# A hybrid-attention layer on one core: a later place in the order for the joining copies, gate units spread anew over the heads, and the last head's weights transposed on TensorE

## The chip, the core and the metric

One core of one Trainium2 chip runs the whole layer as one program. The metric is the device time of one execution in microseconds (us); lower is better. In the profile, PE is TensorE (PEld its weight loads), ACT is ScalarE, DVE is VectorE, POOL is GpSimd and SP is SyncE, whose queue issues most of the DMA transfers. Each engine works through its own list of instructions in order.

## The reference, cut to what matters

The input `x` has 512 rows of 2048 features. One combined projection of the normalised input gives queries, keys, values and a SiLU gate path for three branches of four heads each (head width 128), and merge gates of width 2048 for each branch.

```python
def hybrid_layer(x, norm_g, w_in, ...):
    hn = rmsnorm(x, norm_g)
    proj = jnp.einsum('bsd,dc->bsc', hn, w_in)
    br = proj[..., :QKVG_COLS].reshape(b, s, N_BRANCH, 4, BRANCH_W)
    gates = jax.nn.sigmoid(proj[..., QKVG_COLS + N_HEADS:] + b_gate).reshape(b, s, N_BRANCH, D_MODEL)
    ya = forgetting_attention(rmsnorm(q), rmsnorm(k), v, f_logit)       # branch A: causal softmax with a forget bias
    yb = chunked_relpos_attention(rmsnorm(q), rmsnorm(k), v, rel_bias)  # branch B: softmax over a band
    yc = stick_breaking_attention(q, k, v)                              # branch C: causal, in log space
    ys = jnp.stack([from_heads(ya), from_heads(yb), from_heads(yc)], axis=2)
    ys = ys * jax.nn.silu(br[:, :, :, 3])
    up = jnp.einsum('bsnw,nwd->bsnd', ys, w_up)
    merged = jnp.sum(gates * up, axis=2)
    return x + jnp.einsum('bsd,de->bse', merged, w_out)
```

In each head the attention weights `p` (512 queries by up to 512 keys, in blocks of 128 by 128, of which ten lie on or below the diagonal) are multiplied with the values. On TensorE that product needs the weights with the keys on the partitions, so the ten blocks have to be transposed.

## The kernel before, in words

**Numbers.** All matrix products work on float32 values split into a high and a low part (`split`, L246 to L255: a copy on ACT, L249, and a subtraction on DVE, L253), and three products of parts stand for one.

**Units.** TensorE's work is a stream of units (`stream`): a unit loads 512 KB of weights into a `raw` tile (one of six), splits it into a `w` tile and runs eight matmuls of 512 columns (`mm` in L268, high part) and eight of 256 columns (low part) against the prepared input. Seven units form a `PairTask`: a scheme that saves one product in eight and gives two 128-row results. Each unit's result in PSUM is taken out by ACT or DVE (`after_of`: `u` in L786 and L807, `v` in L790, `c` in L840), and until that is done the matmuls of a unit that needs the same PSUM bank wait. First come the units of the input projection: for each head seven for its queries and keys, then what the table `HEADS` lists behind the head: `g` seven units of merge gates, `s` seven of SiLU gates, `v` fourteen of values. Then come the up-projection (`up_units`) and the output projection (`out_pair`).

**A head's attention** runs beside these units, as small tasks that are started some units behind the head's first one (`OFF`): norms of q and k (`normed`: on ACT and DVE, with one matmul), four score blocks (`soft_scores`, or `stick_scores` in branch C), and for the transposition of the weights two steps around a DMA:

- `apart(i)`, four times: ACT sorts the block row's 16-bit halves (L1200), and SP issues `i + 1` transposing DMAs (L1204), ten in a head. They read and write 16-bit words, so high and low halves of a float32 arrive apart.
- `together(j)`, four times: ACT joins the halves to float32 again (L1213), one key block at a time, once the transposing DMAs into that block's tile have landed; then the result is split for the product with the values.

`av` (L1340 to L1342) multiplies with the values. Tiles of 128 by 512 come from a pool of 20 (`t2s`). A head's `turn()` waits until the head before it has reached its split.

**What sets the order.** The order of the instructions on PE, ACT and DVE is written out by a planner at build time (`Flow`): every task yields the engine and the planned time of its next step, the planner runs all tasks against three planned clocks, and emits a step when it is the earliest that can start. `Event`s carry planned times. For a transposing DMA the planner has no clock of SP: `apart` sets the event `x` of a block row to the planned end of its ACT step plus `XLATE` = 5.0 us (L1206), and `together` becomes possible at the latest of the four. A planned time that the chip does not keep changes no result, but the engine then waits with its whole list behind it. The tasks of a join are costed by `act_us(2 * n)` (L1212).

Of the kernel before, what the change touches and what calls it, by code (L numbers as in the profile page):

```python
# [16 lines left out]
P = 128  # L17
HP = P // 2
S = 512
# [6 lines left out]
QB = S // P  # L26
# [9 lines left out]
A, B, C = 0, 1, 2  # L36
Q, K, V, G = 0, 1, 2, 3
PE, ACT, DVE = 0, 1, 2
# [26 lines left out]
class Flow:  # L65
# [16 lines left out]
    def give(self, slots, n=1):  # L82
        slots.free += [self.fin] * n
# [67 lines left out]
def mm_us(n, x=1):  # L151
    return x * max(0.115, n / 2400 + 0.0133)


def act_us(n, x=1):
    return x * (0.075 + 0.00095 * n)
# [7 lines left out]
def hybrid_kernel(  # L164
# [15 lines left out]
    nc = tc.nc  # L180
# [17 lines left out]
    flow = Flow()  # L198
    spawn, set_, give = flow.spawn, flow.set, flow.give
    t2s, atts, raws, xps = Slots(NT, KEPT), Slots(4), Slots(NR), Slots(NX)  # L200
    accs = [Slots(2), Slots(1), Slots(1)]

    def t2(s, dt=F32):
        return tp.tile([P, S], dt, tag="t2", name=nm(s))
# [14 lines left out]
    def blk(i):  # L219
        return slice(i * P, (i + 1) * P)  # L220
# [52 lines left out]
    def landing(ready, kb):  # L273

        line[0] = max(line[0], ready) + 0.5
        line[1] = max(line[1], line[0] + 1.0) + kb / (340.0 if line[1] < 60.0 else 370.0)
        return line[1] + 1.5

    def fetch(to, src, ready, kb, queue=nc.sync, pinned=False):
        i = queue.dma_start(to, src)  # L280
        if pinned or len(first) < N_FIRST and queue is nc.sync:
            first.append(tc.keep_in_program_order(i))
        return Event(landing(ready, kb))
# [33 lines left out]
    identf = cp.tile([P, P], F32, name="identf")  # L317
# [737 lines left out]
        return [t[0], t[1][:, :S - P], t[2][:, :S - 2 * P], t[1][:, S - P:]]  # L1055

    heads = []

    class Head:
        def __init__(self, n, h, last=False):  # L1060
# [55 lines left out]
        def plain(self, r):  # L1116
# [7 lines left out]
            yield from split(*self.c[r], c, S, self.event("p", r))  # L1124
            give(t2s)

        def soft_start(self):
            n = self.n
            yield from self.turn()
            yield t2s, 4  # L1130
            if n == A:
                yield f2_ev
                self.bias = t2("cb")
                nc.sync.dma_start(self.bias, fd2[self.h:self.h + 1, :].partition_broadcast(P))
                yield Event(landing(flow.now, 256))
                yield DVE, 1.3
                nc.vector.tensor_tensor_scan(self.bias, zeroc.to_broadcast([P, S]), self.bias, 0.0,
                                             op0=ALU.add, op1=ALU.subtract)
                set_(self.event("b"))
            else:  # L1140
                self.bias = t2("tb")
                ev = fetch(self.bias, rel[self.h], flow.now, 256)
                yield ev
                yield DVE, 0.15
                nc.vector.memset(self.bias[0:64, S - 64:], NEG)
                set_(self.event("b"))
            self.p, self.pt = tri("p")[::-1], tris[-1]

        def soft_scores(self, i):
            n = self.n  # L1150
            m = (i + 1) * P
            for e in (("p", Q), ("p", K), ("b",)):
                yield self.event(*e)
            yield atts, 1
            (qh, ql), (kh, kl) = self.c[Q], self.c[K]
            yield PE, mm_us(m, 3)
            ps = att()[:, :m]
            mm3(ps, qh[:, blk(i)], ql[:, blk(i)], kh[:, :m], kl[:, :m], True, True)
            p = self.p[i]
            if n == A:  # L1160
                if i < QB - 1:
                    yield self.event("m", i + 1)
                yield DVE, dve_us(P)
                nc.vector.tensor_add(self.bias[:, blk(i)], self.bias[:, blk(i)], mska)
            mx, sm = small("mx"), small("sm")
            done = self.nth("s", QB)
            yield DVE, dve_us(m) + 0.15
            nc.vector.tensor_tensor_reduce(out=p, in0=ps, in1=self.bias[:, :m] if n == A else self.bias[:, S - m:],
                                           scale=1.0, scalar=-3e38, op0=ALU.add, op1=ALU.max, accum_out=mx)
            nc.vector.tensor_scalar_mul(mx, mx, -1.0)  # L1170
            give(atts)
            set_(self.event("m", i))
            yield ACT, act_us(m) + 0.25
            nc.scalar.activation(p, p, AF.Exp, bias=mx, accum_out=sm)
            if done:
                give(t2s)
                set_(self.event("q"))
            yield DVE, 0.16
            nc.vector.reciprocal(sm, sm)
            yield ACT, act_us(m) + 0.1  # L1180
            nc.scalar.activation(p, p, AF.Copy, scale=sm)
            yield from self.apart(i)

        def apart(self, i):

            m = (i + 1) * P
            up = self.n != A
            if self.nth("x", 1):
                yield self.event("q")
                self.u = t2("u")  # L1190
                self.tt = [t.bitcast(U16).rearrange("p (h q) -> p h q", h=2) for t in tri("tt")]
                set_(self.event("ut"))
            yield self.event("ut")
            if i != (0 if up else QB - 1):
                yield self.event("apart", i - 1 if up else i + 1)
            t0, t1, t2_ = self.pt
            at, to = ((0, self.u), (P, self.u), (0, t2_), (0, t1))[i] if up else                 ((0, t2_), (0, t1), (0, t0), (0, self.u))[i]
            words, u = self.p[i].bitcast(U16), to[:, at:at + m].bitcast(U16)
            yield ACT, act_us(2 * m)
            nc.scalar.activation(u.rearrange("p (j h c) -> p j h c", h=2, c=P),  # L1200
                                 words.rearrange("p (j c h) -> p j h c", h=2, c=P), AF.Copy)
            set_(self.event("apart", i))
            for j in range(i + 1):
                nc.sync.dma_start_transpose(out=self.tt[j][:, :, (i - j) * P:(i - j + 1) * P],  # L1204
                                            in_=u[:, 2 * j * P:2 * (j + 1) * P])
            self.event("x", i).t = flow.fin + XLATE  # L1206

        def together(self, j):
            for i in range(QB):
                yield self.event("x", i)  # L1210
            n, w = S - j * P, self.p[QB - 1 - j]
            yield ACT, act_us(2 * n)  # L1212
            nc.scalar.activation(w.bitcast(U16).rearrange("p (q h) -> p h q", h=2), self.tt[j], AF.Copy)  # L1213
            set_(self.event("w", j))
            for i in range(QB):
                yield self.event("w", i)
            if self.nth("hl6", 1):
                yield t2s, 2
                for k in range(3):
                    h, lo = pair_of("a")  # L1220
                    self.hl[k] = [t[:, :S - k * P] for t in (h, lo)]
                    if k == 1:
                        self.hl[3] = [t[:, S - P:] for t in (h, lo)]
                    set_(self.event("hl", k))
            yield self.event("hl", 2)
            yield from split(*self.hl[j], w, n, self.event("a", j))
            if self.nth("w", QB):
                give(t2s, 3)
# [125 lines left out]
        def stages(self):  # L1354

            s, t = (OFF["s1"], OFF["t1"]) if self.last else (OFF["s"], OFF["t"])
            v, o = (OFF["v1"], OFF["av1"]) if self.last else (OFF["v"], OFF["av"])
            one = lambda fn, i: lambda: fn(i)
            if self.n == C:
                g = [(0, one(self.plain, K)), (0, one(self.plain, Q)), (OFF["cs"] - 2, self.stick_start)]  # L1360
                g += [(OFF["cs"] + i, one(self.stick_scores, i)) for i in range(QB)]
                g += [(OFF["ct"] + i, one(self.together, i)) for i in range(QB)]
            else:
                g = [(0, one(self.normed, K)), (1, one(self.normed, Q)), (s - 2, self.soft_start)]
                g += [(s + i, one(self.soft_scores, QB - 1 - i if self.n == A else i)) for i in range(QB)]
                g += [(t + i, one(self.together, i)) for i in range(QB)]
            return g, [(v, self.value), (o - 3, self.silu), (o, self.av)]


# [148 lines left out]
    first_head(C, 0)  # L1518
    for n, h, more in HEADS:
        last_head = head(n, h, more, (n, h) == (A, NH - 1))  # L1520
# [267 lines left out]
    for k in range(UK):  # L1788
# [13 lines left out]
NR = 6  # L1802

VLATE = 1.0
XLATE = 5.0
ONTO = {6: 1, 7: 6, 4: 7, 3: 5}
HEADS = [(C, 1, "gg"), (C, 2, "sgg"), (C, 3, "gv"), (B, 0, "sgg"), (B, 1, "ggg"), (B, 2, "sgg"), (B, 3, "gv"),
         (A, 0, "sg"), (A, 1, "gg"), (A, 2, "sgg"), (A, 3, "ggggg")]

OFF = dict(cs=3, ct=12, s=11, t=17, v=1, av=8, s1=8, t1=13, v1=0, av1=3, fb=24, a0=11, b0=23)  # L1810

# [55 lines left out]
```

## Time and profile before

| what | value |
|---|---|
| median of 3 runs (lowest to highest) | 1335.48 us (1335.48 to 1337.04) |
| the profiled execution, its own time | 1337.29 us |
| its span, first to last instruction | 1335.4 us |
| DVE, ACT and POOL busy | 1146.0 us (86%), 891.2 us (67%), 107.1 us (8%) |
| data moved by DMA | 283.55 MB, mean 212 GB/s |

How to read it: busy times are sums over the span for each engine, engines work side by side, and only what ends last at each point sets the time. The profiled execution took 1.8 us longer than the median of the three runs; its span leaves out 1.9 us around the first and the last instruction.

### The profile page before, as it was taken

To read this page: it belongs to the slowest core of one execution; us is meant where nothing else is said; L and a number is where in the kernel's file an instruction comes from. 1 tells how busy PE (TensorE), PEld (TensorE's weight loads), DVE (VectorE), ACT (ScalarE), POOL (GpSimd) and SP (SyncE) were. 2 spreads that over 40 slices of the span, in tenths; PEclk is the share of its full clock that TensorE was granted. 3 is DMA by queue.
4 is the path that set the end of the run, shared out by engine and by line. 5 is a ranking of instruction groups with operands and counts; after the bars stand their busy time and mean duration, and the time that the engine had idled before them with its cause. 6 is when DMAs were issued, how large, how long until landed. Compare 5 with 4: busy or idle time off the path is not lost. (4 is left out here: it accounts for less than half of the span.)

```text
span 1335.4 us, 20240 instructions
## 1 busy us (share of the span) xinstructions
PE 1302.4 (98%) x7237; PEld 1135.2 (85%) x7237; DVE 1146.0 (86%) x1693; ACT 891.2 (67%) x1388; POOL 107.1 (8%) x138
## 2 busy tenths in 40 slices
PE   9999999999999998999999999999898999999999
PEld 6888888888888887887888888888787888898888
DVE  8989878888898797998978989989896988897786
ACT  8887767758676757766677586776876655454443
POOL 0200000002000010100200000100000000000100
PEclk9999999999999899999999999999999999999999
DMA  9979796879869787778878778797778855768883
GB/s 333 243 186 255 184 235 167 235 195 222 242 194 185 208 210 210 188 207 189 208 189 233 211 186 231 179 239 198 190 208 248 292 199 168 205 180 256 240 244 102
DMA packets 135300, 283.55 MB, mean 212 GB/s; under 512 B 46224, under 2 KB 54416, under 8 KB 135200
## 3 DMA queue, kind: packets, MB, share of 16 engines
q1 hardware_dynamic: 114080, 217.97, 51.0%
q0 software_dynamic: 17376, 59.78, 26.2%
q10 hardware_dynamic: 3744, 4.52, 0.9%
q8 instruction: 57, 0.93, 0.3%
q14 instruction: 43, 0.35, 0.1%
HBM read 249.92 MB, written 24.42 MB: 205 GB/s over the span
## 5 line engine op out<-in xcount | busy, mean ns | idle before, releaser
L253 DVE TENSOR_TENSOR w<-raw,w 128x1024 fp32r<-128x1024 f32 (+2 forms) x424 | 500.0, 1184 | 125.9 <-ACT w L249 123.1
L249 ACT ACTIVATE w<-raw 128x1024 fp32r<-128x1024 f32 (+2 forms) x424 | 433.8, 1026 | 183.6 <-PE acc L268 83.2
L268 PE MATMUL acc<-x,w 128*128 128x512 f32 (+1 forms) x2656 | 499.9, 339 | 0.0
L268 PEld LDWEIGHTS acc<-x,w 128*128 128x128 f32 x2656 | 425.7, 190 | 65.6 <-issue 3.0
L268 PE MATMUL acc<-t,w 128*128 128x256 f32 (+1 forms) x1920 | 370.6, 345 | 24.6 <-ACT u L807 12.9
L268 PEld LDWEIGHTS acc<-t,w 128*128 128x128 f32 x1920 | 300.5, 195 | 61.9 <-ACT u L807 13.7
L268 PE MATMUL acc<-m,w 128*128 128x256 f32 (+1 forms) x960 | 157.3, 326 | 0.3 <-DVE m L253 0.3
L268 PEld LDWEIGHTS acc<-m,w 128*128 128x128 f32 x960 | 141.3, 190 | 16.3 <-DVE m L253 0.5
L286 POOL DMA_DIRECT2D raw<-in_w_col x80 | 69.2, 865 | 813.8 <-DMA raw<-in_w_col 234.3
L268 PE MATMUL att<-y,w 128*128 128x512 f32 x384 | 89.6, 389 | 0.0
L268 PEld LDWEIGHTS att<-y,w 128*128 128x128 f32 x384 | 72.1, 188 | 14.9
L268 PE MATMUL acc<-w,x 128*128 128x512 f32 (+1 forms) x336 | 62.6, 337 | 0.0
L786 ACT ACTIVATE u<-acc 128x512 f32<-128x512 f32 x50 | 29.8, 595 | 48.0 <-PE acc L268 43.1
L647 DVE TENSOR_TENSOR raw<-raw,raw 128x1024 f32<-128x1024 f32 x48 | 58.5, 1220 | 0.2
L653 DVE TENSOR_TENSOR raw<-raw,raw 128x1024 f32<-128x1024 f32 x48 | 58.5, 1218 | 0.1
L268 PEld LDWEIGHTS acc<-w,x 128*128 128x128 f32 x336 | 52.1, 190 | 6.7
L807 ACT ACTIVATE u<-acc 128x512 f32<-128x512 f32 x49 | 29.1, 593 | 38.5 <-PE acc L268 35.1
L527 DVE TENSOR_TENSOR c<-c,begin_in 128x512 f32<-128x512 f32 x80 | 54.4, 685 | 0.0
L840 ACT ACTIVATE c<-acc 128x256 f32<-128x256 f32 x49 | 18.6, 380 | 52.3 <-PE acc L268 48.0
L1213 ACT ACTIVATE p<-tt 128x1024 uint16<-128x1024 uint16 (+3 forms) x32 | 27.3, 916 | 37.6 <-DMA tt<-p 29.4
L790 ACT ACTIVATE v<-acc 128x512 f32<-128x512 f32 x53 | 31.5, 594 | 25.8 <-PE acc L268 24.7
L726 DVE TENSOR_TENSOR c<-u 128x256 f32<-128x256 f32 x105 | 44.0, 424 | 3.0
(212 smaller groups left out, 1380.5 us busy)
## 6 DMA issues: line engine op xcount, KB each, us to landing
raw<-in_w_col SPq DMA_DIRECT2D x200, 512.0 KB, 4.5
raw<-in_w_col POOLq DMA_DIRECT2D x80, 512.0 KB, 6.3
raw<-in_w_out SPq DMA_DIRECT2D x40, 512.0 KB, 5.0
raw<-in_w_v SPq DMA_DIRECT2D x24, 512.0 KB, 6.2
gl<-c SPq DMA_DIRECT2D x48, 256.0 KB, 4.1
raw<-in_w_up SPq DMA_DIRECT2D x32, 384.0 KB, 3.9
sg<-gl SPq DMA_DIRECT2D x48, 256.0 KB, 4.5
raw<-in_w_out POOLq DMA_DIRECT2D x16, 512.0 KB, 6.0
```

Source lines behind the costliest of these rows:

```text
L249: nc.scalar.activation(hi, src, AF.Copy)
L253: nc.vector.tensor_sub(lo, src, f(hi))
L268: nc.tensor.matmul(ps, w, x, start=start, stop=stop, skip_group_check=more)
L286: i = nc.gpsimd.dma_start(to, src, accum_op=ALU.add)
L527: nc.vector.tensor_mul(c, c if src is None else src, rstd[0][:c.shape[0], :])
L647: nc.vector.tensor_add(w[1], w[1], w[5])
L653: nc.vector.tensor_add(w[2], w[2], w[1])
L726: add(to, src[:, LH], src[:, RH])
L786: nc.scalar.activation(self.u, ps, AF.Copy)
L790: nc.scalar.activation(self.v, ps, AF.Copy)
L807: nc.scalar.activation(self.s, ps, AF.Copy)
L1213: nc.scalar.activation(w.bitcast(U16).rearrange("p (q h) -> p h q", h=2), self.tt[j], AF.Copy)
```

## The change

Four things change, and all the rest of the program follows from the planner's tables.

1. **When a join is planned.** A running time `turned` stands for SP: a block row's transposing DMAs are planned to be issued one after the other, 1.3 us each, behind those of the rows before, and `XLATE` is 8.0 us instead of 5.0. The event `x` takes that time.
2. **What a join is planned to cost**: 0.16 + 0.0024 n us on ACT instead of `act_us(2 * n)`, where n is 512, 384, 256 or 128.
3. **The table `HEADS`**: 23 `g`, 5 `s` and 2 `v` entries as before, but some of the gate groups stand behind other heads.
4. **The last head** (branch A, head 3) no longer uses `apart` and `together`. Its softmax leaves `p` as it is, and `soft_trans(j)` transposes the blocks of one key block on TensorE into one PSUM tile, from which `split` reads. The four tiles that went over to `apart` before are given back.

```diff
--- before.py
+++ after.py
@@ -1055,6 +1055,7 @@
         return [t[0], t[1][:, :S - P], t[2][:, :S - 2 * P], t[1][:, S - P:]]
 
     heads = []
+    turned = [0.0]
 
     class Head:
         def __init__(self, n, h, last=False):
@@ -1124,6 +1125,32 @@
             yield from split(*self.c[r], c, S, self.event("p", r))
             give(t2s)
 
+        def parts_of(self, j):
+
+            if j < 3:
+                yield t2s, 2
+                h, lo = pair_of("a")
+                self.hl[j] = [t[:, :S - j * P] for t in (h, lo)]
+                if j == 1:
+                    self.hl[3] = [t[:, S - P:] for t in (h, lo)]
+                set_(self.event("hl", j))
+            else:
+                yield self.event("hl", 1)
+
+        def soft_trans(self, j):
+            for i in range(QB):
+                yield self.event("s", i)
+            yield from self.parts_of(j)
+            yield atts, 1
+            yield PE, 0.11 * (QB - j)
+            ps = att()
+            for i in range(j, QB):
+                nc.tensor.transpose(ps[:, blk(i)], self.p[i][:, blk(j)], identf)
+            if self.nth("t", QB):
+                give(t2s, 3)
+            yield from split(*self.hl[j], ps[:, j * P:], S - j * P, self.event("a", j))
+            give(atts)
+
         def soft_start(self):
             n = self.n
             yield from self.turn()
@@ -1173,13 +1200,16 @@
             yield ACT, act_us(m) + 0.25
             nc.scalar.activation(p, p, AF.Exp, bias=mx, accum_out=sm)
             if done:
-                give(t2s)
+                give(t2s, 5 if self.last else 1)
                 set_(self.event("q"))
             yield DVE, 0.16
             nc.vector.reciprocal(sm, sm)
             yield ACT, act_us(m) + 0.1
             nc.scalar.activation(p, p, AF.Copy, scale=sm)
-            yield from self.apart(i)
+            if self.last:
+                set_(self.event("s", i))
+            else:
+                yield from self.apart(i)
 
         def apart(self, i):
 
@@ -1203,13 +1233,14 @@
             for j in range(i + 1):
                 nc.sync.dma_start_transpose(out=self.tt[j][:, :, (i - j) * P:(i - j + 1) * P],
                                             in_=u[:, 2 * j * P:2 * (j + 1) * P])
-            self.event("x", i).t = flow.fin + XLATE
+            turned[0] = max(turned[0], flow.fin + 0.3) + 1.3 * (i + 1)
+            self.event("x", i).t = turned[0] + XLATE
 
         def together(self, j):
             for i in range(QB):
                 yield self.event("x", i)
             n, w = S - j * P, self.p[QB - 1 - j]
-            yield ACT, act_us(2 * n)
+            yield ACT, 0.16 + 0.0024 * n
             nc.scalar.activation(w.bitcast(U16).rearrange("p (q h) -> p h q", h=2), self.tt[j], AF.Copy)
             set_(self.event("w", j))
             for i in range(QB):
@@ -1363,7 +1394,7 @@
             else:
                 g = [(0, one(self.normed, K)), (1, one(self.normed, Q)), (s - 2, self.soft_start)]
                 g += [(s + i, one(self.soft_scores, QB - 1 - i if self.n == A else i)) for i in range(QB)]
-                g += [(t + i, one(self.together, i)) for i in range(QB)]
+                g += [(t + i, one(self.soft_trans if self.last else self.together, i)) for i in range(QB)]
             return g, [(v, self.value), (o - 3, self.silu), (o, self.av)]
 
 
@@ -1802,10 +1833,9 @@
 NR = 6
 
 VLATE = 1.0
-XLATE = 5.0
+XLATE = 8.0
 ONTO = {6: 1, 7: 6, 4: 7, 3: 5}
-HEADS = [(C, 1, "gg"), (C, 2, "sgg"), (C, 3, "gv"), (B, 0, "sgg"), (B, 1, "ggg"), (B, 2, "sgg"), (B, 3, "gv"),
-         (A, 0, "sg"), (A, 1, "gg"), (A, 2, "sgg"), (A, 3, "ggggg")]
+HEADS = [(C, 1, "g"), (C, 2, "sgg"), (C, 3, "v"), (B, 0, "sggg"), (B, 1, "gg"), (B, 2, "sggg"), (B, 3, "gv"), (A, 0, "s"), (A, 1, "ggg"), (A, 2, "sggg"), (A, 3, "ggggg")]
 
 OFF = dict(cs=3, ct=12, s=11, t=17, v=1, av=8, s1=8, t1=13, v1=0, av1=3, fb=24, a0=11, b0=23)
```

Between a head's last L1200 copy and its first join, ACT's list has these numbers of weight splits (`w<-raw`, one in each unit), for the heads in the order in which they run. Before: 2, 3, 3, 5, 2, 3, 3, 2, 3, 2, 1, 2. Now: 5, 6, 6, 6, 7, 7, 6, 6, 6, 5, and 5 in the eleven heads that still join. (In the changed program the L1200 copy is L1230 and the join L1244.)

**Place 1: ACT in the second head (branch C, head 1).** Before, from the last sorting copy (L1200) on; `z` and `tt` are the weights and their transposed halves, `acc` the PSUM bank of a unit, `u` and `c` what is taken out of it:

```order
L1200 ACTIVATE z_1597<-z_1596 128x1024
L249 ACTIVATE w_1944<-raw_1838 128x1024
L249 ACTIVATE w_1971<-raw_1875 128x1024
L840 ACTIVATE c_293_1955<-acc_1796 128x256
L249 ACTIVATE w_1992<-raw_1838 128x1024
L1213 ACTIVATE z_1596<-tt_1767 128x2x512
L1213 ACTIVATE z_1597<-tt_1768 128x2x384
L786 ACTIVATE u_2019<-acc_1993 128x512
L249 ACTIVATE w_2020<-raw_1706 128x1024
```

Now, from the same copy on:

```order
L1230 ACTIVATE z_1577<-z_1576 128x1024
L249 ACTIVATE w_1944<-raw_1838 128x1024
L249 ACTIVATE w_1971<-raw_1875 128x1024
L840 ACTIVATE c_293_1955<-acc_1796 128x256
L249 ACTIVATE w_1992<-raw_1838 128x1024
L786 ACTIVATE u_2015<-acc_1993 128x512
L249 ACTIVATE w_2016<-raw_1706 128x1024
L249 ACTIVATE w_2043<-raw_1888 128x1024
L807 ACTIVATE u_2015<-acc_1993 128x512
L249 ACTIVATE w_2068<-raw_1875 128x1024
L1244 ACTIVATE z_1576<-tt_1767 128x2x512
L790 ACTIVATE v_2092<-acc_2069 128x512
```

The first join has moved behind three more weight splits, and the two copies that take a unit out of PSUM, `u` in L786 and `u` in L807, now stand ahead of it.

**Place 2: ACT in branch A, head 2, while head 3's queries and keys are normed.** Before; `rs` comes from DVE and `qkh` is the high part of a normed query or key:

```order
L249 ACTIVATE w_9638<-raw_9308 128x1024
L1200 ACTIVATE p_9264<-p_9263 128x256
L477 ACTIVATE rw_9603<-rt_9602 128x512
L249 ACTIVATE w_9665<-raw_9481 128x1024
L249 ACTIVATE qkh_9673<-rs_9528 128x512
L786 ACTIVATE u_9637<-acc_9608 128x512
L1213 ACTIVATE p_9262<-tt_9476 128x2x512
L1213 ACTIVATE p_9263<-tt_9477 128x2x384
```

Now:

```order
L840 ACTIVATE c_1467_9566<-acc_9398 128x256
L249 ACTIVATE w_9605<-raw_9434 128x1024
L477 ACTIVATE rw_9612<-rt_9611 128x512
L1244 ACTIVATE p_9252<-tt_9362 128x2x512
L786 ACTIVATE u_9640<-acc_9606 128x512
L249 ACTIVATE w_9641<-raw_9334 128x1024
L1244 ACTIVATE p_9253<-tt_9363 128x2x384
L1244 ACTIVATE p_9254<-tt_9364 128x2x256
L1244 ACTIVATE p_9253<-tt_9363 128x2x128
L249 ACTIVATE qkh_9650<-rs_9524 128x512
```

Before, the copy `u` in L786 stood behind `qkh`; now it stands behind the first join, and `qkh` comes five rows later.

**Place 3: the last head, on ACT and PE.** Before, ACT had the sorting copies, two splits, the joins, and the copy `u` in L807 behind the first join:

```order
L1200 ACTIVATE p_9920<-p_9921 128x512
L1200 ACTIVATE p_9921<-p_9920 128x256
L786 ACTIVATE u_10118<-acc_10086 128x512
L249 ACTIVATE w_10119<-raw_9775 128x1024
L249 ACTIVATE w_10144<-raw_9929 128x1024
L1213 ACTIVATE p_9919<-tt_10031 128x2x512
L807 ACTIVATE u_10118<-acc_10086 128x512
```

Now ACT reads the transposed weights out of PSUM; L1208 is the last step of the softmax (the weights by the reciprocal of their sum):

```order
L1201 ACTIVATE p_9958,sm_10157<-p_9958,mx_10156 128x128
L249 ACTIVATE w_10197<-raw_10102 128x1024
L1208 ACTIVATE p_9958<-p_9958,sm_10157 128x128
L249 ACTIVATE ah_10213<-att_10229 128x512
L249 ACTIVATE ah_10215<-att_10234 128x384
L249 ACTIVATE ah_10217<-att_10240 128x256
L249 ACTIVATE w_10249<-raw_9979 128x1024
L249 ACTIVATE ah_10215<-att_10243 128x128
```

On PE the ten transposes stand in one piece inside a unit's low part, between two of its matmuls; `p` are the weights, `identf` is a 128 by 128 identity in float32:

```order
L268 MATMUL acc_10140<-x_14_122,w_10139 128x256
L1148 MATMUL att_10229<-identf,p_9958 128x128
L1148 MATMUL att_10229<-identf,p_9959 128x128
L1148 MATMUL att_10229<-identf,p_9958 128x128
L1148 MATMUL att_10229<-identf,p_9957 128x128
L1148 MATMUL att_10234<-identf,p_9959 128x128
L1148 MATMUL att_10234<-identf,p_9958 128x128
L1148 MATMUL att_10234<-identf,p_9957 128x128
L1148 MATMUL att_10240<-identf,p_9958 128x128
L1148 MATMUL att_10240<-identf,p_9957 128x128
L1148 MATMUL att_10243<-identf,p_9957 128x128
L268 MATMUL acc_10140<-x_15_123,w_10139 128x256
```

Nothing stood there on PE before; ten instructions are added and none is taken away on that engine.

## The prediction

> **What bounds the kernel now.** I read the page's busy times first, then the granted clock, then who PE waited for, because an engine that is busy nearly all the time leaves only its own idle time and its own slow time to win.
>
> ```profile
> PE 1302.4 (98%) x7237; PEld 1135.2 (85%) x7237; DVE 1146.0 (86%) x1693; ACT 891.2 (67%) x1388; POOL 107.1 (8%) x138
> core 0: 1335.4 us, clock 0.991
> PE acc L268 <- ACT u L807: 12.9, 4, 4.8
> PE acc L268 <- ACT u L786: 11.5, 5, 3.7
> PE att L1101 <- DVE sq L253: 2.7, 1, 2.7
> PE att L1341 <- DVE vl L253: 1.1, 1, 1.1
> PE acc L268 <- DVE m L253: 0.3, 1, 0.3
> ```
>
> PE is the bound: 1302.4 of 1335.4 us. What is left is 33 us of idle time and a clock that was 0.9% short on average, 12.0 us of the span. Nearly all the idle time stands in nine waits for ACT's copies out of PSUM (12.9 and 11.5 us) and one for a DVE result. So I laid a window of 12 us from the start of each long wait, to see idle time and clock together; the columns after the window are its length, then busy time of PE, PEld, DVE, ACT and POOL, then the granted clock, DMA share and GB/s.
>
> ```profile
> 183.00:195.00 12.00, 9.69 (x49) 8.31 (x48) 6.63 (x10) 9.78 (x16) 0.70 (x2) 0.86 0.89 261
> 433.00:445.00 12.00, 8.82 (x37) 7.44 (x36) 5.72 (x8) 9.12 (x13) 0.87 (x1) 0.72 0.98 247
> 527.00:539.00 12.00, 8.25 (x42) 7.16 (x41) 8.52 (x12) 10.55 (x18) 0.87 (x1) 0.86 0.88 285
> 615.00:627.00 12.00, 8.70 (x44) 7.40 (x43) 9.01 (x13) 9.36 (x15) 0.87 (x1) 0.86 0.82 234
> 697.00:709.00 12.00, 9.99 (x56) 8.53 (x55) 8.05 (x11) 11.85 (x22) 0.86 (x1) 1.00 0.99 306
> 795.00:807.00 12.00, 9.30 (x50) 7.83 (x50) 9.29 (x12) 11.81 (x20) 1.73 (x2) 1.00 0.97 267
> 953.00:965.00 12.00, 8.29 (x42) 7.12 (x41) 7.86 (x12) 7.05 (x10) 0.04 (x1) 0.86 0.97 256
> 1007.00:1019.00 12.00, 7.22 (x33) 6.21 (x32) 3.40 (x5) 8.26 (x13) 0.87 (x1) 0.86 0.69 212
> ```
>
> Twelve minus PE's busy time is PE's idle time: 2.31, 3.18, 3.75, 3.30, 2.01, 2.70, 3.71 and 4.78 us, 25.7 us in all. In six of the eight windows the clock is down as well: 0.14 of 12 us is 1.7 us lost, 0.28 is 3.4 us, together 11.8 us. That is the whole of the missing clock (12.0 us): each long wait is paid twice.
>
> Who makes ACT late is in the timeline of the last of them and in ACT's own waits.
>
> ```profile
> 997.98 1.06 ACT L1200 ACTIVATE p<-p 128x512 uint16<-128x512 uint16 x2
> ...
> 1005.26 2.46 SPq L1204 DMA_TRANSPOSE tt<-p  x2
> 1007.82 0.53 SPq L1381 DMA_DIRECT2D gl<-c  x1
> 1008.44 1.18 SPq L1204 DMA_TRANSPOSE tt<-p  x1
> ...
> 1010.74 1.34 ACT L1213 ACTIVATE p<-tt 128x1024 uint16<-128x1024 uint16 x1 [7.43 <-DMA tt<-p]
> ...
> 1011.95 0.56 ACT L807 ACTIVATE u<-acc 128x512 f32<-128x512 f32 x1
> ...
> 1012.57 0.80 PE L268 MATMUL acc<-t,w 128*128 128x256 f32 x2 [4.78 <-ACT u L807]
> ```
>
> ```profile
> ACT p L1213 <- DMA tt<-p: 29.4, 9, 7.4
> ACT p L1213 <- issue: 8.3, 2, 5.3
> ACT z L1213 <- DMA tt<-z: 4.8, 3, 3.0
> DVE sq L253 <- ACT sq L249: 5.0, 1, 5.0
> ```
>
> ACT reached its first join 7.43 us before the transposed halves had landed. SP issues the transposing DMAs one by one, about 1.2 us each, so the tenth went out 9.4 us after the last sorting copy had ended (999.04), and the join started 11.7 us after it. The copy `u` of L807 stood behind the join, and PE stood behind `u` for 4.78 us. Over the program ACT waits 42.5 us for such halves; where the list has `u`, or the split of `sq` (the wait of 2.7 us at 795), close behind a join, PE waits too. Seven of the eight windows are of this kind, 22.0 us idle. The one at 953 is not:
>
> ```profile
> 955.30 0.75 DVE L1109 SCALAR_TENSOR_TENSOR rs<-rs,gq,c 128x512 f32<-128x512 f32 x1
> ...
> 956.08 0.63 ACT L249 ACTIVATE qkh<-rs 128x512 fp32r<-128x512 f32 x1 [1.45 <-DVE rs L1109]
> 956.62 0.58 ACT L786 ACTIVATE u<-acc 128x512 f32<-128x512 f32 x1
> ```
>
> There ACT waited for DVE's `rs`, and `u` stood behind `qkh`.
>
> **The change part by part.** *The joins' later place.* What decides is how much of ACT's list lies between a head's last sorting copy and its first join. A weight split stands there once a unit, and a unit's sixteen matmuls set its pace:
>
> ```profile
> 985.45 13.98 PE acc L268 x80
> ```
>
> Eighty matmuls are five units: 2.8 us each. Before, the lists have one to three splits there (five in one head), up to 8.4 us; now they have five to seven, 14 to 19.6 us. The head above needed 11.7 us. Its place alone would thus cover it, with 2 us to spare at the least, as ACT's other work only adds distance. What hides the joins is then the units' own work. I count all seven waits as gone: **22.0 us** idle and, from the windows at 183, 433, 527, 615 and 1007 (0.84 of 12 us), **10.1 us** of clock. After that DVE is late next: with 1146.0 us of work in some 1300 it is 88% busy.
>
> *The place at 953.* In the changed list `u` stands ahead of `qkh`, behind a join whose halves are due by the same count. I take the wait as gone, **3.7 us and 1.7 us** of clock; if DVE is late there in another way, up to 5.4 us stay.
>
> *The planned cost of a join* and *the moved gate groups* add and remove no instruction. They only shift steps, and every other wait may come or go with that. Before, small waits of this sort are the rows with 1.1 and 0.3 us and what the two rows on `u` hold beyond the windows; the largest single one without a join is the 3.7 us at 953. The bound on one side is nothing (or a gain of the 2 to 3 us of small waits that are there now), on the other two or three new waits like that at 953, each with its 1.7 us of clock: 11 to 16 us. I take **3 us**, nearer to the small rows, as one such wait came in twelve heads before.
>
> *The last head on PE.* Ten instructions are added to the engine that bounds, each of 128 columns of float32. The nearest rows:
>
> ```profile
> 978.13 0.06 PE att L1340
> 978.20 0.11 PE att L1341
> L515 PE MATMUL att<-dg,tmpc 128*128 128x512 f32 x2 | 1.0, 590 | 0.0
> ```
>
> A matmul of 128 columns of split parts takes PE 0.06 to 0.11 us. L515 is the one product in plain float32 of that width of weights, and it took two instructions and 1.0 us for 512 columns, 0.25 us for 128. So the ten cost 0.6 to 2.5 us; I take **2.0 us**, nearer to L515, since identity and weights are plain float32 like its operands. ACT loses four sorting copies and four joins and SP ten issues, all beside PE. The added wait is PE's: the first transpose waits for the softmax's last scaling on ACT (L1208), with the rest of the unit behind it. Before, PE had no such wait; ACT's list has one weight split between the last exponential and that scaling, so a PE that comes early pays about a microsecond, which is inside the 3 us.
>
> The Trainium skill ("TensorE: Matmul & The Clock Gate", Part 4: PE-mode transpose) speaks against this part: it puts such a transpose at about 275 ns inside a kernel, and says that the clock gate does not count it as PE being busy. By that page the ten would take an estimated 2.75 us, 0.75 more than I take, and could bring a halved window of 1.7 us. The trace cannot show a transpose; it shows that 2.70 us idle at 795 left the clock at 1.00 and 2.31 us at 183 did not, so a stretch of that length can go either way. The same page (Part 1) names an idle window of about 3.4 us as what closes the gate; the wait of 2.31 us shows that less can do.
>
> *The sum.* Against the profiled execution: 22.0 + 10.1 + 3.7 + 1.7 - 3 - 2.0 = 32.5 us less than its 1337.29, so 1304.8. The median of the runs lies 1.8 us under that execution and its waits belong to the same order, so the same 32.5 us from 1335.48 give **1303 us**.
>
> **The rivals.**
>
> *New in-order waits eat part of it.* Later joins bring later splits and later products with the values, and on DVE, at 88%, several steps then stand close together. For it: the wait at 953 came from just such a crowd, and the wait of 1.1 us for `vl` from another. Against it: they are the only two of their kind in twelve heads. Three waits like that at 953 (5.4 us each) instead of my 3 us: 1303 + 13 = 1316 us.
>
> *The joins still wait.* SP's list is in order too: if stores and loads among the transposing DMAs hold them back, halves land later than 14 us after the last copy in some heads. For it: 0.53 us went to a store between the transposes above. Against it: ACT's place would have to be missed by over 2 us in every head. Half of the seven waits back (16 us): 1319 us.
>
> *Slower than before.* A head's halves, weights and split results lie in up to thirteen of the pool's twenty tiles, and they are now held for three or four units longer. If the copies out of PSUM then wait for a tile, PE waits in each of the eleven heads. For it: the windows show the price of a long wait, 4.8 + 1.7 us at 1007. Against it: no wait of PE before is put down to a tile. It decides from 3.0 us a head on (32.5 / 11); at 6.5 us in seven of the heads it takes 45 us: 1303 + 45 = 1348 us.
>
> *The clock counts the transposes as idle*, by the mechanism that halved it at 183: one window more, 1.7 us, and 0.5 us for transposes at the upper bound: 1305 us. The page of the Trainium skill named above has this as its rule.
>
> **How the numbers follow.** Chances: forecast 0.56, the clock's rival 0.10 (both at 1296 to 1310), new waits 0.18, joins still waiting 0.07, a result within 0.2%, where these two add up, 0.04, slower 0.05. The lower end of the range is all waits and all clock gone but PE's start, with the transposes at their lower bound: 1335.5 - 25.7 - 11.8 - 2.8 of small waits + 0.6 = 1296. The upper end takes in the two rivals on this side: 1319. Some 0.13 is left out above, and little below. A difference under 0.2% (2.7 us) cannot be told from no change here; so faster 0.91, same 0.04, slower 0.05.
>
> **What would show it.** In the changed profile, the joins' rows should have no wait for `tt` of over a microsecond, the rows of PE waiting for `u` in L786 and L807 (now at later lines) should fall from 24.4 us to a few, the clock should read 0.998 or more, and PE's busy time should be 98% or 99% of a span of about 1301 us. Ten transposes should take about 2 us in one piece. The prediction is wrong if ACT still waits at the joins, if the clock still drops six times, or if PE's idle time has moved to waits for DVE.

## The result and the profile after

| kernel | median | lowest to highest | runs |
|---|---|---|---|
| before | 1336.91 us | 1335.48 to 1343.77 | 6 |
| after | 1307.35 us | 1305.54 to 1309.78 | 6 |

The ratio is 0.977, with a 95% interval of 0.9744 to 0.9796: 29.6 us less, where 32.5 us less had been forecast. The median lies 4.4 us above the predicted 1303. Of these, 2.9 us are the smaller difference, and 1.4 us come from the kernel before, which took 1336.91 us in this comparison and not the 1335.48 us the sum started from.

The page of the kernel after, its core's clock, and whom PE waited for (in total us, times, longest):

```profile
PE 1294.0 (99%) x7247; PEld 1128.8 (86%) x7247; DVE 1144.7 (88%) x1693; ACT 883.8 (68%) x1380; POOL 106.8 (8%) x138
core 0: 1305.6 us, clock 0.999
PE acc L268 <- ACT u L807: 3.2, 3, 1.8
PE acc L268 <- DVE w L253: 1.8, 3, 0.7
PE att L1811 <- POOL nhepsc L313: 1.1, 1, 1.1
PE acc L268 <- ACT v L790: 1.0, 1, 1.0
PE acc L268 <- ACT w L249: 0.6, 1, 0.6
PE acc L268 <- DVE m L253: 0.3, 1, 0.3
```

The waits for `u` have gone from 24.4 us to 3.2, the clock from 0.991 to 0.999. PE now works 99% of its span. The groups of joins show why (busy time, mean ns of one, idle time just before them), first the softmax heads' before the change, then both groups after it:

```profile
L1213 ACT ACTIVATE p<-tt 128x1024 uint16<-128x1024 uint16 (+3 forms) x32 | 27.3, 916 | 37.6 <-DMA tt<-p 29.4 <-issue 8.3
...
L1244 ACT ACTIVATE p<-tt 128x1024 uint16<-128x1024 uint16 (+3 forms) x28 | 24.1, 921 | 0.0
L1244 ACT ACTIVATE z<-tt 128x1024 uint16<-128x1024 uint16 (+3 forms) x16 | 13.8, 920 | 0.0
```

Each join costs ACT what it did before, but none of the 44 waits. Of the 42.5 us that the prediction counted as waiting for halves, the profile puts 34.2 down to a DMA and 8.3 to nothing it shows ("issue"); both have become 0.0. ACT waits for other transfers now:

```profile
ACT w L249 <- DMA raw<-in_w_col: 30.8, 12, 5.1
...
ACT y L1347 <- DMA g<-gd: 4.4, 1, 4.4
```

Before, the first row read 0.6 us, once, and the second was not there. The second leads to the longest wait that PE still has. Three pieces of the timeline, of SP's queue, of ACT and of PE (start, length, idle time before and its releaser in brackets):

```profile
653.64 5.05 SPq L1234 DMA_TRANSPOSE tt<-p  x4
658.74 0.58 SPq L280 DMA_DIRECT2D g<-gd  x1
```

```profile
664.95 0.63 ACT L1347 ACTIVATE y<-g 128x512 f32<-128x512 f32 x1 [4.40 <-DMA g<-gd]
665.61 0.63 ACT L1349 ACTIVATE y<-y 128x512 f32<-128x512 f32 x1
666.14 0.58 ACT L807 ACTIVATE u<-acc 128x512 f32<-128x512 f32 x1
```

```profile
666.78 1.51 PE L268 MATMUL acc<-t,w 128*128 128x256 f32 x9 [1.81 <-ACT u L807]
```

It is the old pattern at a new place: the load of `g` (the stored SiLU gate) stood on SP behind four transposing DMAs of 5.05 us, ACT's list held `u` behind the `y` that waits for `g`, and PE paid twice. The load went out at 658.74, and loads of `g` took 5.8 to 6.4 us to land. The window around it and the one around the ten transposes (columns as in the prediction's windows):

```profile
661.00:673.00 12.00, 10.19 (x46) 8.40 (x45) 4.22 (x6) 8.02 (x12) 0.86 (x1) 0.86 0.99 335
984.00:996.00 12.00, 12.00 (x72) 10.62 (x71) 10.93 (x17) 7.43 (x14) 0.86 (x1) 1.00 0.94 281
```

The first shows 1.81 us idle and 0.14 of 12 us, 1.7 us, of clock: nearly all the clock that is still missing. The second has no idle time and a full clock, with the transposes in it:

```profile
L1148 PE MATMUL att<-identf,p x10: 272/273/273, 988.4 to 989.4; 128*128 128x128 f32 x10
```

One takes 272 to 273 ns from its start to its end (lowest, median, highest; the profile models the ends of matmuls), but all ten start within about 1 us, 0.11 us from one to the next.

**Where the 29.8 us between the two spans come from.** PE's waits over the trace: 29.7 before, 8.2 after, 21.5 less (the rows of waits, rounded, add up to 29.6 and 8.0). Missing clock: 12.0 us before, 1.7 after, 10.3 less. Ten transposes: 1.1 us more. These sum to 30.7, and 0.9 us of it are too much. About half of that is time counted twice: the slow clock of the window at 433 began 1 us before PE's wait ended, and half of such idle time was counted as lost clock too. The rest stays open.

### The profile page after: what moved, and what is told of

The parts are those of the page before. It is cut to its first block, busy times and chain, and to the rows that moved or that the text cites. A ratio compares the mean times of both kernels' runs of the same rounds, so it can differ in the third digit from the quotient of the medians.

```text
span 1305.6 us, 20205 instructions
## 1 busy us (share of the span) xinstructions
PE 1294.0 (99%) x7247; PEld 1128.8 (86%) x7247; DVE 1144.7 (88%) x1693; ACT 883.8 (68%) x1380; POOL 106.8 (8%) x138
## 4 chain that ended last, share of the span: by engine, by line
PE 85%; DVE 5%; DMA 5%; ACT 3%; issue 1%; SPq 0%; ACTq 0%; POOL 0%; DVEq 0%; POOLq 0%
PE acc L268 71%; PE att L268 10%; DMA raw<-in_w_col 3%; DVE w L253 2%; ACT w L249 1%; DMA raw<-in_w_v 1%; PE att L264 1%; PE att L265 1%; PE att L263 1%; PE att L1372 1%; PE att L1373 1%; PE att L1371 0%; DMA g<-gd 0%; SPq L1234 0%; ACT p L1244 0%
## 5 line engine op out<-in xcount | busy, mean ns | idle before, releaser
L268 PE MATMUL acc<-t,w 128*128 128x256 f32 (+1 forms) x1920 | 360.7, 339 | 4.6 <-ACT u L807 3.2
L268 PEld LDWEIGHTS acc<-t,w 128*128 128x128 f32 x1920 | 293.4, 191 | 40.2 <-ACT u L807 3.8
L786 ACT ACTIVATE u<-acc 128x512 f32<-128x512 f32 x50 | 29.8, 595 | 39.6 <-PE acc L268 34.6
L807 ACT ACTIVATE u<-acc 128x512 f32<-128x512 f32 x49 | 29.0, 592 | 39.2 <-PE acc L268 38.8
L268 PE MATMUL acc<-y,w 128*128 128x512 f32 x192 | 46.1, 389 | 0.0
L840 ACT ACTIVATE c<-acc 128x256 f32<-128x256 f32 x49 | 18.5, 378 | 40.1 <-PE acc L268 32.5
```

Source lines behind the costliest of these rows:

```text
L268: nc.tensor.matmul(ps, w, x, start=start, stop=stop, skip_group_check=more)
L786: nc.scalar.activation(self.u, ps, AF.Copy)
L807: nc.scalar.activation(self.s, ps, AF.Copy)
L840: nc.scalar.activation(c, ps[:, RH], AF.Copy, scale=-1.0)
```

## The experiments

The theory: the joins came before their halves, ACT's list held PE's copies behind them, and their later place alone is worth the gain. The rivals: the new order of gate groups carries it; the last head carries it; or any later place brings other waits. Times are medians (lowest to highest); each ratio is against the kernel before, run beside it. The kernel after (ratio 0.9744 to 0.9796) was not run beside these kernels, so differences to it are between sets of runs.

### The joins' later place alone

The kernel before, with only this (all twelve heads still by DMA, the old table):

```diff
-            self.event("x", i).t = flow.fin + XLATE
+            turned[0] = max(turned[0], flow.fin + 0.3) + 1.3 * (i + 1)
+            self.event("x", i).t = turned[0] + XLATE
-XLATE = 5.0
+XLATE = 8.0
```

> Kernel before with one part alone: the joins' planned time (running time for SP, 8.0 us behind it). Theory: the joins' place in ACT's list made the waits, so this part alone brings nearly all of the gain: no ACT wait for transposed halves over 1 us in any of the twelve heads, PE idle time from 28 to 5-10 us, clock 0.998 or more, 26 to 31 us less than before (about 1308). Rival (the gate groups' new spread is needed, since later joins without it make new waits on PE): joins' waits gone, but new PE waits of 10 us or more, 12 to 18 us less than before (about 1320).

Measured: 1322.15 us (1321.34 to 1324.44), ratio 0.9887 (0.986 to 0.9914), 15.9 us less than the 1338.01 beside it. Its joins, its clock, whom PE waited for, and one row of ACT's waits:

```profile
L1215 ACT ACTIVATE p<-tt 128x1024 uint16<-128x1024 uint16 (+3 forms) x32 | 27.7, 923 | 0.0
core 0: 1320.1 us, clock 0.994
PE att L1342 <- ACT vh L249: 7.7, 1, 7.7
PE acc L268 <- DVE v L811: 4.7, 1, 4.7
PE acc L268 <- ACT u L786: 2.2, 1, 2.2
PE att L268 <- ACT y L249: 1.4, 1, 1.4
...
ACT y L249 <- DMA yr<-yd: 7.6, 3, 4.9
```

The mechanism held, for no join waits, and the theory's size fell; the rival's 12 to 18 us less was met, though most of the waits stand at the last head. PE is idle for 19.2 us, and 14.7 of them lie between 1003 and 1033, at the end of the gate units. The last head has no later units to lie beside, so its late joins push its product with the values into the up-projection, and PE waits 7.7 us for the copy `vh` of the reloaded values. The 4.7 us at 1003 have another cause: ACT waited 4.93 us for `yr` (stored results, reloaded for the up-projection), whose loads stood on SP behind five transposing DMAs of the last head (6.32 us).

### The last head on PE alone, and the new table alone

The kernel before with only `soft_trans` and `parts_of` for the last head, as in the change's diff:

> Kernel before with one part alone: the last head's weights transposed on TensorE. Theory: only the last of the long waits goes (4.8 us and 1.7 us of clock), ten transposes add 1.1 us, so 5 us less than before (about 1331); the other joins wait as before. Rival (transposes on TensorE cost as much as they win, or the softmax's tail makes PE wait instead): within 1.5 us of before.

Measured: 1335.1 us (1329.34 to 1339.21), ratio 0.9976 (0.9958 to 0.9994), 2.9 us less. The wait of 4.78 us at 1007 is gone; the profiled execution is idle for 29.7 us all the same, since waits at other joins stayed or grew, as at 526 (5.17) and 798 (4.48).

The kernel before with only the new `HEADS`:

> Kernel before with one part alone: the gate groups' new spread over the heads. Theory: the joins stay planned 5 us behind the last sorting copy, so the waits stay, if at other heads: PE idle 22 to 32 us, within 6 us of before. Rival (the spread removes waits by itself, as at 953): 10 us or more less than before.

Measured: 1345.81 us (1344.83 to 1346.99), ratio 1.006 (1.0038 to 1.0081): 7.8 us slower. PE is idle for 36.7 us and the joins wait as before. ACT's rows of waits for halves, of the first kernel and of the second:

```profile
ACT p L1243 <- DMA tt<-p: 29.0, 8, 5.5
```

```profile
ACT p L1213 <- DMA tt<-p: 31.6, 7, 6.6
```

Neither of these two parts makes the gain by itself. The three, each alone, sum to 15.9 + 2.9 - 7.8 = 11.0 us less. The whole change has 29.6. The joins' planned cost was not tried alone.

### The change without its new table, and without its last head

The kernel after with the table of before:

```diff
-HEADS = [(C, 1, "g"), (C, 2, "sgg"), (C, 3, "v"), (B, 0, "sggg"), ...
+HEADS = [(C, 1, "gg"), (C, 2, "sgg"), (C, 3, "gv"), (B, 0, "sgg"), ...
```

> Changed kernel with one part undone: the gate groups stand as before. Theory (joins' place carries the gain): within 4 us of the changed kernel (1304 to 1311), the wait for DVE's rs in branch A head 2 gone too if the joins' place removed it. Rival (the spread carries part of it): 1316 or more, with a long PE wait again where head 3 of branch A is normed.

Measured: 1315.89 us (1314.54 to 1317.93), ratio 0.9837 (0.9814 to 0.986), 8.5 us above the kernel after, with intervals that do not overlap. The rival was right. No join waits; PE waits for `u` in two places of branch A's heads, at 884 (5.27) and 936 (4.24):

```profile
PE acc L268 <- ACT u L786: 9.5, 2, 5.3
```

```profile
888.64 0.63 ACT L1355 ACTIVATE y<-y 128x512 f32<-128x512 f32 x1 [2.48 <-DVE y L1353]
889.17 0.58 ACT L786 ACTIVATE u<-acc 128x512 f32<-128x512 f32 x1
```

At 884 ACT waited for DVE, with `u` behind it. That is the kind of wait that stood at 953 before. With the joins 8.0 us behind and the old table such waits are there; with the new table they are not.

The kernel after with its last head by DMA, too:

```diff
-                g += [(t + i, one(self.soft_trans if self.last else self.together, i)) for i in range(QB)]
+                g += [(t + i, one(self.together, i)) for i in range(QB)]
```

> Changed kernel with the last head by DMA again (sorting copies, transposing DMAs, joins), the rest as changed. Theory (from the run with the later joins alone): the last head's later joins push its product with the values behind the end of the gate units, so PE waits 10 us or more between 985 and 1030 us: 12 to 22 us above the changed kernel. Rival (the tail came from the old gate spread): within 5 us of the changed kernel.

Measured: 1322.27 us (1320.1 to 1327.92), ratio 0.9875 (0.9832 to 0.9917), about 15 us above the kernel after. PE's waits at the last head, at 1006 and 1030, and one row of ACT's:

```profile
PE acc L268 <- ACT s L807: 6.6, 1, 6.6
...
PE att L1368 <- ACT vh L249: 3.1, 1, 3.1
...
ACT y L249 <- DMA yr<-yd: 8.2, 5, 6.6
```

No join waits here, and the larger wait does not come from the late product. In the profiled execution, which took 1327.92 us, SP issued the last six transposing DMAs of the head from 997.54 to 1005.18, and the loads of `yr` only from 1005.89 on. ACT waited 6.59 us for them, until 1008.56, and the copy `s`, which takes a unit out of PSUM, came behind at 1011.87. PE went on at 1012.50. The 3.1 us at 1030 are the late product with the values.

So the last head on PE is worth about 15 us inside the whole change and 2.9 us alone. With the old table and the joins later it is worth 6.3 us, together with the joins' planned cost (1322.15 to 1315.89). It takes the last ten transposing DMAs off SP, where the reloads for the up-projection need the queue.

### What ten transposes cost

The kernel after, each transpose done eight times over, 80 in one piece:

```diff
+            for _ in range(8):
                 for i in range(j, QB):
                     nc.tensor.transpose(ps[:, blk(i)], self.p[i][:, blk(j)], identf)
```

> Changed kernel with the last head's ten transposes on TensorE issued eight times over (eighty in one piece, the same result). Theory (the clock counts a transpose as work): 70 more at 0.11 us each, 7.7 us more than the changed kernel, the clock at 1.00 in the windows around them. Rival (transposes count as idle): at least one halved window of 3.4 us within 7 us of their start, 1.7 us or more on top, and transposes at 0.22 us each in it.

One run, 1313.79 us, 6.4 us above the kernel after, where 7.7 us had been expected. Its transposes, and the window around them:

```profile
L1149 PE MATMUL att<-identf,p x80: 272/272/273, 987.2 to 995.9; 128*128 128x128 f32 x80
```

```profile
983.00:997.00 14.00, 14.00 (x112) 13.35 (x111) 5.92 (x8) 4.56 (x9) 0.86 (x1) 1.00 0.77 223
```

Eighty stand in 8.7 us, 0.11 each, and the clock stayed at 1.00 throughout. The clock's rival is out. The rule of the Trainium skill ("TensorE: Matmul & The Clock Gate", Part 4: PE-mode transpose) fits in its 275 ns, if these are read as the time from start to end of one (272 in the profile); that the gate does not count transposes as work does not agree with this window.

### How late the joins have to be

First with a constant in place of SP's running time, then with the running time and less behind it:

```diff
-            turned[0] = max(turned[0], flow.fin + 0.3) + 1.3 * (i + 1)
-            self.event("x", i).t = turned[0] + XLATE
+            self.event("x", i).t = flow.fin + XLATE
-XLATE = 8.0
+XLATE = 13.0
```

> Changed kernel without the running time for SP: each block row's joins are planned a constant 13 us behind its own sorting copy. Theory (only the distance matters): joins land in time as with the running time, within 4 us of the changed kernel. Rival (the serial time is needed): ACT waits for transposed halves come back in heads whose copies stand close together, with two or more long PE waits, 10 us or more on top.

```diff
-XLATE = 8.0
+XLATE = 3.0
```

> Changed kernel with 3.0 us instead of 8.0 us behind the running time. In the changed kernel the first join came 8 to 11 us after the last transposing DMA's issue; now 3 to 6 us are left, and a DMA takes 4 us to land. Theory (lateness at the joins makes the waits, with a threshold): ACT waits for halves come back in part, 3 to 12 us in all, the time 2 to 12 us above the changed kernel. Rival (8.0 is more than needed and only holds tiles longer): no ACT wait for halves over 1 us and the time the same or up to 4 us lower.

The constant: 1319.77 us (1316.45 to 1322.8), ratio 0.9861 (0.9823 to 0.9899). No join waits, and PE is idle for 14.6 us in waits of another kind, the longest 3.35 us at 939. The shorter delay: 1313.92 us (1308.88 to 1317.07), ratio 0.9814 (0.9773 to 0.9855). Joins came 1.6 to 6.1 us after the last issue on SP and waited 0.2, 1.6 and 0.6 us in all; the long waits of PE are 2.69, 2.45 and 2.20 us at 871, 933 and 957, in branch A's heads and not at joins. Neither expectation met the case: any distance that covers the transfers frees the joins, and what is left differs by where everything else comes to lie. The time of the shorter delay can't be told from the kernel after, as the intervals of their ratios overlap. Why these two orders have just these waits stays open.

### One planned clock for SP's loads and transposes

In the kernel after, the planner's running time for transposes is apart from the one (`line`) by which it places SP's loads. Here they share it; in the second kernel with `XLATE = 5.0`:

```diff
-            turned[0] = max(turned[0], flow.fin + 0.3) + 1.3 * (i + 1)
-            self.event("x", i).t = turned[0] + XLATE
+            line[0] = max(line[0], flow.fin + 0.3) + 1.3 * (i + 1)
+            self.event("x", i).t = line[0] + XLATE
```

> Changed kernel, with the transposing DMAs put on the same planned line of SP as the loads and stores, so that a load behind them is planned late too (its joins still 8.0 us behind). Theory (the waits that are left come from loads that stand behind transposing DMAs on SP): ACT's waits for DMA loads in the gate units fall from 37 us to under 15, PE idle from 8.2 to 5 us or less, 2 to 6 us under the changed kernel (about 1303). Rival (what is left is crowding of ACT and DVE, which any new order deals anew): ACT's waits for loads stay or only shift, PE idle 6 to 15 us, 1305 to 1318.

> As the run with one planned line for SP, but the joins 5.0 us behind it. Theory (the line then carries SP's lateness, and tiles come free sooner): as that run within 3 us, no ACT wait for halves over 1 us. Rival (crowding): 1308 to 1318, as the run with 3.0 us.

With 8.0: 1319.67 us (1319.29 to 1322.83), ratio 0.9861 (0.9821 to 0.9901). The wait for `g` is gone and ACT waits 18.2 us for weights instead of 30.8, yet PE's idle time rose to 18.8 us. At 518:

```profile
522.06 0.63 ACT L249 ACTIVATE qkh<-rs 128x512 fp32r<-128x512 f32 x1 [3.18 <-DVE rs L1110]
522.60 0.58 ACT L786 ACTIVATE u<-acc 128x512 f32<-128x512 f32 x1
```

```profile
510.00:524.00 14.00, 8.56 (x46) 7.27 (x45) 13.97 (x21) 10.36 (x18) 0.89 (x2) 0.97 0.90 221
```

DVE works 13.97 of 14 us, `rs` comes late, and `u` stands behind the copy that needs it. The rival held: crowding on DVE. With 5.0: 1342.01 us (1335.95 to 1347.24), ratio 1.002 (0.9995 to 1.0045), no gain at all over the kernel before. Its joins, and a window at its longest wait:

```profile
L1244 ACT ACTIVATE p<-tt 128x1024 uint16<-128x1024 uint16 (+3 forms) x28 | 23.7, 920 | 0.0
```

```profile
940.00:955.00 15.00, 7.75 (x43) 6.60 (x42) 13.89 (x33) 8.83 (x17) 0.01 (x1) 0.81 0.64 177
```

No join waits here either; PE is idle for 31.3 us in 22 waits, none of them at a join. This run is the plainest of all: joins in time are not enough. That they are needed is argued and not shown: the three kernels whose joins wait for tens of us take 1335 to 1346 us, but the whole change with only its joins early was not run.

### What ACT waits for now

The kernel after with the weights of all eight softmax heads transposed on PE, so that 70 transposing DMAs fewer stand on SP:

```diff
-                g += [(t + i, one(self.soft_trans if self.last else self.together, i)) for i in range(QB)]
+                g += [(t + i, one(self.soft_trans, i)) for i in range(QB)]
```

> Changed kernel with the weights of all eight softmax heads (branches A and B) transposed on TensorE, seven heads more. Seventy transposes more at 0.11 us are 7.7 us of PE; SP loses seventy transposing DMAs, ACT 56 copies. Theory (SP's transposing DMAs make loads late, and that is most of the small waits): the waits in the second half of the gate units go, 3 us or less of idle there, so 1307 + 8 - 5 = 1310, at most 1312. Rival (waits left over are crowding on DVE and ACT): they stay, 1313 to 1320.

Measured: 1310.63 us (1310.36 to 1311.28), ratio 0.9786 (0.9754 to 0.9818). ACT's waits for weights fell from 30.8 to 2.7 us:

```profile
ACT w L249 <- DMA raw<-in_w_col: 2.7, 1, 2.7
```

With these DMAs gone, the loads come in time. The DMAs alone do not make them late: the kernel before has ten more of them than the kernel after, and its ACT waited 0.6 us for weights. PE's idle time is 6.2 us, 2.0 less, but PE has 70 transposes more, 7.7 us at 0.11, and that outweighs it.

Last, the kernel after with only the six loads of `g` moved to ACT's queue:

```diff
-                yield fetch(g, d, flow.now, 256)
+                yield fetch(g, d, flow.now, 256, nc.scalar)
```

> Changed kernel with six loads (a SiLU head's stored gates, g<-gd) issued from ACT's queue instead of SP's; PE's and DVE's lists stay the same, row for row. Theory (the one long wait that is left, 1.8 us at 665 with its halved clock, comes from such a load behind four transposing DMAs on SP): that wait and the clock's drop go, 1 to 4 us under the changed kernel (1304 to 1306), ACT's wait of 4.4 us for g gone. Rival (ACT's own issue and its waits for a free tile cost as much): within 1 us of the changed kernel or slower.

Measured: **1303.53 us** (1302.97 to 1305.03), ratio 0.974 (0.9708 to 0.9771). The same window as above, and the clock:

```profile
661.00:673.00 12.00, 12.00 (x70) 10.54 (x69) 7.27 (x10) 10.16 (x14) 0.87 (x1) 1.00 1.01 344
core 0: 1302.9 us, clock 1.000
```

The load of `g` now goes out at 647.02, 11.7 us earlier, and these loads land in 2.9 to 4.7 us. PE no longer waits there and the clock no longer drops. It is the fastest kernel of the study, with all its runs under the lowest of the kernel after; the two were not run side by side, and the intervals of their ratios overlap. The wait at 665 and its halved window were 3.5 us in the profiled execution, and the medians differ by 3.8. That need not be the whole account, as the clock reads 1.000 in three of the six runs of the kernel after, so that not every run had the halved window.

## Why the prediction was right, and where it was off

- **The mechanism** (joins ahead of their halves, `u` behind them, idle time and clock paid together) held: no kernel with later joins loses more than 2.4 us before them, the one with 3.0 us of delay, and the others lose nothing. Its "42.5 us for such halves" holds 8.3 us that the profile puts down to no transfer; they went too.
- **"Its place alone would thus cover it ... I count all seven waits as gone".** True of the joins' waits, and true of the sum only with the other two parts. Alone, the later joins bring 15.9 us and not the 32.1 of the first term (22.0 + 10.1), because the last head's tail then hangs into the up-projection, and its transposing DMAs hold up the reloads there.
- **The place at 953** went, as forecast, but for another reason than the one given ("behind a join whose halves are due by the same count"). With the old table and joins in time, waits for `u` still stand in the same heads, at 936 (the same place, earlier now by the time won until then) with ACT busy, and at 884 behind a late DVE. With the new table and the joins 8.0 us behind they are gone; with the same table and another delay they are back (3.35 us at 939, 2.45 at 933, 5.57 at 948). So it is the two together, and why just these two fit stays open.
- **The moved gate groups at 3 us** is the step that was argued wrongly, though the sum came out close. I costed them as small change around the joins; they carry 8.5 us of the gain. The rows of before could not show it: there the new table alone costs 7.8 us. That 3 us came near is in part luck: seven other orders with later joins were run (the change short of a part, or with another delay or planned clock), and their medians lie 6.6 to 34.7 us above the kernel after, mostly through new waits of the kind to which the prediction gave 0.18.
- **New small waits** were too low: 4.0 us of small waits were to stay (29.7 - 25.7), with 0.2 us of clock (12.0 - 11.8), and 3 us to come; 8.2 us idle and 1.7 us of clock were measured, 2.7 us more. **The transposes** were too high, 1.1 us and not 2.0: each is one instruction of 0.11 us, where the product in L515 took two. And the account of the spans holds 0.9 us too much, as said above. Together: 2.7 - 0.9 + 0.9 = 2.7 us, and the spans differ by 29.8 us, 2.7 short of the forecast 32.5.
- **"After that DVE is late next"** holds of the orders that failed (the windows at 510 and 940, DVE 13.97 of 14 and 13.89 of 15 us busy). In the kernel after it was SP: its longest wait came from a load behind transposing DMAs. I had named SP's queue only as a danger to the joins, not to the loads behind them.
- **The rival of new in-order waits** described a real danger, at about its price: with the table of before two long waits come, and 1315.89 us, where the rival had three and 1316. It was not what this change does. **Tiles held longer** did not show in any row of PE's waits.

## What to carry to other kernels

An instruction that needs a transfer belongs in its engine's list behind enough other work to cover the whole issue of that transfer on its queue, not only its landing; look then at what stands behind the transfers on that queue. In a planned order the parts of a change don't add up: the last head's part was worth 2.9 us or 15, the table 7.8 us slower or 8.5 faster, depending on the others, so take each out of the whole too, and don't only put each into the old kernel. After each gain read the list of waits anew: the longest one left named the next edit, one word, worth about 4 us.

## What was not expected of the hardware

- Transposes of 128 by 128 float32 on PE go through at 0.11 us each while the profile gives each 272 ns, and 80 in a row leave the clock at 1.00.
- The clock's answer to a wait goes not by its length alone: 1.81 us at 665 halved it for 3.41 us, 1.85 us at the same place in the run with 80 transposes did not, nor did 2.70 us at 795 before the change. What decides is where the wait falls. The slow stretches begin on a fixed grid: before the change at 186.50, 435.67, 531.25, 619.99, 957.91 and 1012.53, each a whole number of 3.413 us from the others. Cut by the grid of its trace, the wait at 665 puts 1.81 us into one stretch; the other two fall to 1.57 and 0.28, and to 1.79 and 0.90. Over all fourteen traces, each of the 35 full-speed stretches with 2.0 us or more of idle PE is followed by a halved one, and none of those with less than 1.45 us is; in between it is 5 of 20. So whether a wait of some 2 us is paid twice is in part chance.
